# Expert weights of a PEER layer built for groups of 16 tokens instead of 8, in single one-hot tiles of twice the size and with a third PSUM bank

## The chip, the cores and the metric

The kernel runs on one core of one Trainium2 chip. The metric is the device time of one execution in microseconds (us), as the median of several runs. Engines: PE is TensorE (matmul; PEld is its weight load), DVE is VectorE, ACT is ScalarE, POOL is GpSimd, SP is SyncE, which issues the loads. Each engine works through its own queue in order; which order that is, a scheduler decides when the program is built, from the order in the source, the buffers and its own estimates.

## What is computed

One layer of a hybrid decoder for 256 tokens of width 1024. First an attention part, then the PEER part that the change touches: 8 heads choose 16 experts each out of 16384 for every token, and expert `e` adds `weight * gelu(h . u_e) * v_e`:

```
e_idx = jnp.take_along_axis(cand_idx, pos, axis=-1)
g = jax.nn.softmax(g_s, axis=-1)
u = u_emb[e_idx]
act = jax.nn.gelu(jnp.einsum('btd,bthkd->bthk', hc, u).astype(jnp.float32), approximate=False)
return jnp.einsum('bthk,bthkd->btd', (g * act).astype(h.dtype), v_emb[e_idx])
```

The kernel gathers nothing. It forms all 16384 products with U, multiplies each by its weight (zero for nearly all), and sums all 16384 rows of V with that. An expert's number is a pair (i1, i2) of 0 to 127; "row j" below is the set of 128 experts with i2 = j, and there are 128 rows.

## The kernel before

**Up to 240 us**: attention, projections, product keys. Then three stages follow one another on PE.

**The U stage (lines 920 to 954, 240 to 643 us)** takes the 128 rows of U. For row j, `take()` (line 119) gives the row's matrix in two parts: ACT makes `hi` (line 106) and DVE `lo` (line 108) from the loaded `raw` tile, three rows ahead at most, because `hi` and `lo` have three buffers each. PE runs 16 matmuls (lines 942 and 943, eight of 512 and eight of 256 columns) into one bank: `pa` (two buffers), `c1`, `c2` or `c3` in turn. ACT then copies half of the bank to `gt` (line 948), DVE adds the other half (line 949), and ACT applies gelu: straight into the store for tokens that have no weights yet (line 951), and in `gt` for those that have, which DVE then multiplies into the store (lines 953, 954). The store (`storeA`, `storeB`) holds 128 rows of 256 tokens.

**The weights** are built inside the U stage, from row J0 = 32 on, by `weights(g, j)` (line 879) for NQ = 8 tokens at a time, 32 groups in all, one every 2.8 rows. DVE makes two one-hot tiles by comparing an iota with the chosen numbers (`o1`, line 889; `og`, line 890). ACT makes `ol`, one copy per token with the low part of the weight as scale (line 892); these copies read `og`. Only when all of them are through does DVE multiply `og` in place by the high part (line 893). PE then multiplies, for each token, `o1` with `og` and with `ol` (lines 899 and 900, here called the products): 128 by 128 weights per token. Four tokens fill a bank (a quad), taken from `pb`, which has two. Each quad is emptied by DVE for rows that are done (line 905, it multiplies them into the store) and by ACT for the rest (line 907). `o1`, `og` and `ol` have two buffers each.

**The V stage (lines 961 to 996, 643 to 988 us)** takes the 128 rows of V. Each row of the store is split by ACT (`wh`, line 916) and DVE (`wl`, line 917) in `split_row`, whose tiles take the places of `o1`, `og` and `ol` in turn, so that six rows can be split ahead. PE runs 12 matmuls of 512 columns per row (`mm3`, lines 126 to 128). Between rows 4 and 12, eight loads of `w_ada` pass through the same `raw` buffers, and DVE sums them (line 983). The last three rows (125 to 127) are kept for the tail (lines 999 to 1039), which also forms the final norm.

While `sides` (line 759) has work left, DVE also runs the routing of the tokens (lines 761 to 854), up to row 31. What the order of the work around the change rests on is one line, which says at which rows a group is due:

```
while gdone < T // NQ and gdone < (j - J0 + 1) * (T // NQ) / (122 - J0):
```

Of the kernel before, what the change touches and what calls it, by code (L numbers as in the profile page):

```python
# [8 lines left out]
FR = mybir.dt.float32r  # L9
HT = mybir.dt.float16  # L10
# [6 lines left out]
T = 256  # L17
# [3 lines left out]
NEG = -1.0e30  # L21
SENT = -3.0e38
GSCALE = 32768.0
NQ = 8
BUCKET_START = [0, 1, 2, 3, 4, 5, 6, 7, 8, 9, 10, 11, 12, 13, 14, 15, 16, 23, 32, 46, 64, 91, 128, 182]
CAND_N = [16 // (a + 1) for a in range(16)]
CAND_OFF = [sum(CAND_N[:a]) for a in range(16)]
# [14 lines left out]
def hybrid_kernel(ctx, tc, io, out):  # L42
# [3 lines left out]
    def pool(name, bufs=1, stack=ctx, **kw):  # L46
        return stack.enter_context(tc.tile_pool(name=name, bufs=bufs, **kw))
# [6 lines left out]
    def bank(tag, bufs=1):  # L54
        return psum.tile([128, 512], FT, tag=tag, name=tag, bufs=bufs)
# [4 lines left out]
    def bank_b():  # L60
        return bank("pb", 2)
# [26 lines left out]
    def raw_tile():  # L88
        return st.tile([128, 1024], FT, tag="raw", name="raw", bufs=4)
# [66 lines left out]
    for part in (1, 0):  # L156
        for c in range(8):
            w = first_w[part, c] = w0.tile([128, 1024], FT, tag="wada", name="wada", bufs=8)
# [512 lines left out]
    for db in range(8):  # L671
# [4 lines left out]
        for c in range(8):  # L676
            w = slice(c * 128, c * 128 + 128)
# [59 lines left out]
    for c in range(8):  # L737
        w = slice(c * 128, c * 128 + 128)
# [125 lines left out]
    ph = pool("ph")  # L864
# [6 lines left out]
    def pieces(j0, j1):  # L871
        if j0 < SPL:
            yield storeA, j0, j0, min(j1, SPL)
        if j1 > SPL:
            yield storeB, max(j0, SPL) - SPL, max(j0, SPL), j1
# [3 lines left out]
    def weights(g, j):  # L879

        t0 = NQ * g
        sh = [128, NQ // 2, 128, 2]
        o1, og, ol = [ph.tile(sh, HT, tag=n, name=n, bufs=2) for n in ("o1", "og", "ol")]

        def of(x):
            return x[:, t0:t0 + NQ].rearrange("p (a b) -> p a b", b=2)[:, :, None, :].to_broadcast(sh)

        ii = iota[:, None, :, :].to_broadcast(sh)
        nc.vector.tensor_tensor(o1, ii, of(i1T), op=OP.is_equal)
        nc.vector.tensor_tensor(og, ii, of(i2T), op=OP.is_equal)  # L890
        for q in range(NQ):
            nc.scalar.activation(ol[:, q // 2, :, q % 2], og[:, q // 2, :, q % 2], AF.Copy, scale=glT[:, t0 + q:t0 + q + 1])  # L892
        nc.vector.tensor_tensor(og, og, of(ghT), op=OP.mult)
        for q0 in range(0, NQ, 4):
            w = bank_b()
            for q in range(4):
                qs = slice(q * 128, q * 128 + 128)
                a, b = (q0 + q) // 2, (q0 + q) % 2
                nc.tensor.matmul(w[:, qs], o1[:, a, :, b], og[:, a, :, b], start=True, stop=False)  # L899
                nc.tensor.matmul(w[:, qs], o1[:, a, :, b], ol[:, a, :, b], start=False, stop=True)  # L900
            wv = w.rearrange("p (q i) -> p i q", q=4)
            tq = slice(t0 + q0, t0 + q0 + 4)
            for s, a, lo_, hi_ in pieces(0, j):
                dst = s[:, a:a + hi_ - lo_, tq]
                nc.vector.scalar_tensor_tensor(dst, wv[:, lo_:hi_, :], 1.0 / GSCALE, dst, op0=OP.mult, op1=OP.mult)
            for s, a, lo_, hi_ in pieces(j, 128):
                nc.scalar.activation(s[:, a:a + hi_ - lo_, tq], wv[:, lo_:hi_, :], AF.Copy, scale=1.0 / GSCALE)

    def row(j):
        return storeA[:, j, :] if j < SPL else storeB[:, j - SPL, :]  # L910

    def split_row(j):

        w = ph.tile([128, 2, T], FR, tag=("o1", "og", "ol")[j % 3], name="w", bufs=2)
        wh, wl = w[:, 0, :], w[:, 1, :]
        nc.scalar.activation(wh, row(j), AF.Copy)
        nc.vector.tensor_tensor(wl, row(j), wh.bitcast(FT), op=OP.subtract)
        return wh, wl

    for j in range(128):  # L920
# [6 lines left out]
        if j == J0:  # L927
# [3 lines left out]
            storeB = sb_pool.tile([128, 128 - SPL, T], FT, name="storeB")  # L931
        while gdone < T // NQ and gdone < (j - J0 + 1) * (T // NQ) / (122 - J0):
            weights(gdone, j)
            gdone += 1
            done = NQ * gdone
        if j == 126:
            first_rows = [split_row(0), split_row(1)]
        hi, lo = take()
        ps = bank(("pa", "c1", "pa", "c2", "c3")[j % 5], 2 if j % 5 in (0, 2) else 1)
        for c in range(8):  # L940
            w = slice(c * 128, c * 128 + 128)
# [18 lines left out]
    tail = []  # L960
    for j in range(128):
        wh, wl = split_row(j) if j > 1 else first_rows[j]
        hi, lo = take()

# [11 lines left out]
        if 4 <= j < 12:  # L976
            c = j - 4
            w = raw_tile()
# [28 lines left out]
    w = slice(512, 1024)  # L1007
    residual(acc[3], 1, w, x2[:, 1, w])
    for i, (tt, a, n) in enumerate(TAIL):
        w = slice(a, a + n)  # L1010
# [84 lines left out]
```

## Time and profile before

| | |
|---|---|
| median of 3 runs | 1009.87 us (1008.82 to 1010.7) |
| the profiled execution | 1007.38 us, of which its span is 1005.6 us |
| PE busy | 970.1 us (96%) in 5693 matmuls |
| DVE busy | 778.0 us (77%) |
| ACT busy | 635.0 us (63%) |
| loads | 192.78 MB on SP's queue, 58.7% of the 16 DMA engines |
| chain that ended last | PE 63%, DVE 8%, DMA 2%, ACT 2% |
| mean granted TensorE clock | 0.995 |

The span runs from the first to the last instruction; the execution's own time has 1.8 us more around it. A matmul's duration reaches past the start of the next one, since matmuls are pipelined: how fast PE works is read from start to start, and its busy share only says that it was not left waiting for long.

### The profile page before, as it was taken

What the parts mean: (1) busy time and instruction counts of PE and PEld (TensorE: products, weight loads), DVE (VectorE), ACT (ScalarE), POOL (GpSimd) and SP (SyncE); (2) the same over time, 40 slices, a digit from 0 to 9 for tenths busy, and PEclk for the clock granted to TensorE, in tenths of its full rate; (3) what the DMA queues carried; (4) which work ended last, traced back from release to release, by engine and by line L of the source; (5) the groups of instructions that cost most, each with busy time, mean ns of one, the idle gap of its engine ahead of it and who ended that gap; (6) DMA issues with size and microseconds to landing.
All of it is one profiled execution on the core that took longest, in us unless ns stands there. A gap on an engine that the chain in (4) does not pass through costs nothing.

```text
span 1005.6 us, 16222 instructions
## 1 busy us (share of the span) xinstructions
PE 970.1 (96%) x5693; PEld 826.4 (82%) x5693; DVE 778.0 (77%) x1597; ACT 635.0 (63%) x1419; POOL 23.4 (2%) x62
## 2 busy tenths in 40 slices
PE   8899999899899999999999999999999999999996
PEld 6777888898778888888888888887888888888885
DVE  5869979799999988888889898667555555555556
ACT  4565765545556699988889787545445554554453
POOL 0000210003000000000000000000000000000000
PEclk9999999999999999999999999999999999999998
DMA  8964766453455555555555555678655666566551
GB/s 340 391 235 151 252 248 192 164 169 127 150 188 167 186 159 161 168 168 175 164 166 167 167 168 171 236 257 280 204 192 190 193 201 191 190 193 198 194 190 63
DMA packets 54996, 195.15 MB, mean 194 GB/s; under 512 B 6097, under 2 KB 8193, under 8 KB 54530
## 3 DMA queue, kind: packets, MB, share of 16 engines
q1 hardware_dynamic: 54594, 192.78, 58.7%
q10 hardware_dynamic: 320, 1.34, 0.3%
q8 instruction: 45, 0.74, 0.3%
q14 instruction: 37, 0.30, 0.1%
HBM read 191.97 MB, written 2.12 MB: 193 GB/s over the span
## 4 chain that ended last, share of the span: by engine, by line
PE 63%; DVE 8%; DMA 2%; ACT 2%; issue 1%; DVEq 0%; ACTq 0%
PE c L942 11%; PE c L127 10%; PE c L126 10%; PE c L128 10%; PE pa L942 8%; PE c L943 6%; PE pa L943 4%; DVE lo L108 2%; PE pb L899 1%; PE pb L900 1%; DMA raw<-w_ada 1%; ACT hi L106 1%; DVE gt L949 1%; DMA raw<-V 0%; ACT ol L892 0%
## 5 line engine op out<-in xcount | busy, mean ns | idle before, releaser
L108 DVE TENSOR_TENSOR lo<-raw,hi 128x1024 fp32r<-128x1024 f32 x296 | 361.5, 1222 | 170.2 <-ACT hi L106 169.4
L106 ACT ACTIVATE hi<-raw 128x1024 fp32r<-128x1024 f32 x299 | 316.1, 1058 | 222.5 <-PE c L128 151.6
L942 PE MATMUL c<-h,hi 128*128 128x512 f32 x608 | 218.2, 399 | 1.2 <-ACT hi L106 1.2
L127 PE MATMUL c<-lo,w 128*128 128x512 f32 x509 | 198.6, 390 | 1.1 <-DVE lo L108 1.0
L126 PE MATMUL c<-hi,w 128*128 128x512 f32 x509 | 198.4, 390 | 0.0
L128 PE MATMUL c<-hi,w 128*128 128x512 f32 x509 | 198.0, 389 | 0.0
L943 PE MATMUL c<-h,lo 128*128 128x256 f32 x608 | 158.3, 281 | 5.0 <-DVE lo L108 5.0
L942 PE MATMUL pa<-h,hi 128*128 128x512 f32 x416 | 151.7, 399 | 1.0 <-ACT hi L106 1.0
L942 PEld LDWEIGHTS c<-h,hi 128*128 128x128 f32 x608 | 112.8, 188 | 22.8 <-ACT hi L106 2.1
L943 PEld LDWEIGHTS c<-h,lo 128*128 128x128 f32 x608 | 114.0, 189 | 12.6 <-DVE lo L108 7.2
L127 PEld LDWEIGHTS c<-lo,w 128*128 128x128 f32 x509 | 95.5, 188 | 23.0 <-DVE lo L108 3.1
L126 PEld LDWEIGHTS c<-hi,w 128*128 128x128 f32 x509 | 95.5, 188 | 20.4 <-ACT hi L106 0.7
L128 PEld LDWEIGHTS c<-hi,w 128*128 128x128 f32 x509 | 95.5, 188 | 19.8
L943 PE MATMUL pa<-h,lo 128*128 128x256 f32 x416 | 108.6, 281 | 1.0 <-DVE lo L108 1.0
L942 PEld LDWEIGHTS pa<-h,hi 128*128 128x128 f32 x416 | 78.0, 188 | 15.4 <-ACT hi L106 1.4
L892 ACT ACTIVATE ol<-og,glT 128x128 f16<-128x128 f16 x256 | 88.0, 435 | 0.1
L943 PEld LDWEIGHTS pa<-h,lo 128*128 128x128 f32 x416 | 78.1, 189 | 5.8 <-DVE lo L108 2.3
L126 PE MATMUL pa<-h,hi 128*128 128x256 f32 x240 | 70.5, 294 | 4.6 <-ACT h L254 3.3
L128 PE MATMUL pa<-h,lo 128*128 128x256 f32 x240 | 68.4, 285 | 0.7 <-DVE lo L108 0.7
L127 PE MATMUL pa<-h,hi 128*128 128x256 f32 x240 | 68.6, 286 | 0.0
L948 ACT ACTIVATE gt<-c 128x256 f32<-128x256 f32 x76 | 29.0, 381 | 36.5 <-PE c L942 36.2
L126 PEld LDWEIGHTS pa<-h,hi 128*128 128x128 f32 x240 | 46.2, 193 | 6.5 <-ACT h L254 3.6
(284 smaller groups left out, 1380.5 us busy)
## 6 DMA issues: line engine op xcount, KB each, us to landing
raw<-U SPq DMA_DIRECT2D x128, 512.0 KB, 3.5
raw<-V SPq DMA_DIRECT2D x128, 512.0 KB, 4.2
wada<-w_ada SPq DMA_DIRECT2D x40, 512.0 KB, 6.5
raw<-wqk SPq DMA_DIRECT2D x19, 512.0 KB, 5.8
raw<-wq SPq DMA_DIRECT2D x16, 512.0 KB, 4.0
raw<-wv SPq DMA_DIRECT2D x8, 512.0 KB, 8.3
raw<-wo SPq DMA_DIRECT2D x8, 512.0 KB, 4.7
raw<-w_ada SPq DMA_DIRECT2D x8, 512.0 KB, 4.6
```

The lines of the kernel that those rows point to most:

```text
L106: nc.scalar.activation(hi, raw, AF.Copy)
L108: lo_eng.tensor_tensor(lo, raw, hi.bitcast(FT), op=OP.subtract)
L126: nc.tensor.matmul(ps, lh, rh, start=first, stop=False)
L127: nc.tensor.matmul(ps, lh, rl, start=False, stop=False)
L128: nc.tensor.matmul(ps, ll, rh, start=False, stop=last)
L892: nc.scalar.activation(ol[:, q // 2, :, q % 2], og[:, q // 2, :, q % 2], AF.Copy, scale=glT[:, t0 + q:t0 + q + 1])
L899: nc.tensor.matmul(w[:, qs], o1[:, a, :, b], og[:, a, :, b], start=True, stop=False)
L900: nc.tensor.matmul(w[:, qs], o1[:, a, :, b], ol[:, a, :, b], start=False, stop=True)
L942: both = [lambda: nc.tensor.matmul(ps, hi[:, w], hcat[:, c].rearrange("p a t -> p (a t)"), start=(c == 0), stop=(c == 7)), lambda: nc.tens ...
L943: lambda: nc.tensor.matmul(ps[:, T:], lo[:, w], hh[:, c, :], start=False, stop=False)]
L948: nc.scalar.activation(gt, ps[:, T:], AF.Copy)
L949: nc.vector.tensor_tensor(gt, gt, ps[:, :T], op=OP.add)
```

## The change

NQ goes from 8 to 16, so there are 16 groups, one every 5.6 rows, each with 16 copies by ACT and one of each of DVE's three instructions, of 2048 elements instead of 1024. `o1`, `og` and `ol` are twice as large and have one buffer each instead of two, so they take the same room. A group now has four quads, and the third of them goes to bank `c0` instead of `pb`: `pb`, `pb`, `c0`, `pb`. In the V stage `split_row` has one buffer for each of its three tags, so three rows can be split instead of six.

```
-NQ = 8
+NQ = 16
...
-        o1, og, ol = [ph.tile(sh, HT, tag=n, name=n, bufs=2) for n in ("o1", "og", "ol")]
+        o1, og, ol = [ph.tile(sh, HT, tag=n, name=n, bufs=1) for n in ("o1", "og", "ol")]
...
         for q0 in range(0, NQ, 4):
-            w = bank_b()
+            w = bank("c0") if q0 == 8 else bank_b()
...
     def split_row(j):
 
-        w = ph.tile([128, 2, T], FR, tag=("o1", "og", "ol")[j % 3], name="w", bufs=2)
+        w = ph.tile([128, 2, T], FR, tag=("o1", "og", "ol")[j % 3], name="w", bufs=1)
```

The queues of the engines move with it. ACT's queue at the first group, where `ol` are the copies, `gt` and `hi` the work for the U rows, and `storeA` and `storeB` the store. Before:

```order
L951 ACTIVATE storeA<-gt 128x256
L892 ACTIVATE ol<-og,glT 128x128 x8
L948 ACTIVATE gt<-pa 128x256
L106 ACTIVATE hi<-raw 128x1024
L892 ACTIVATE ol<-og,glT 128x128
L951 ACTIVATE storeA<-gt 128x248
L953 ACTIVATE gt<-gt 128x8
L892 ACTIVATE ol<-og,glT 128x128 x2
```

After the change, from the same instruction on:

```order
L951 ACTIVATE storeA<-gt 128x256
L948 ACTIVATE gt<-pa 128x256
L892 ACTIVATE ol<-og,glT 128x128 x16
L951 ACTIVATE storeA<-gt 128x240
L953 ACTIVATE gt<-gt 128x16
L106 ACTIVATE hi<-raw 128x1024
L948 ACTIVATE gt<-c_4126 128x256
```

The eight copies stood ahead of the `gt` of the row in `pa`, and on PE the first products 14 matmuls behind that row. Now all sixteen stand behind that `gt`, in one piece, with the next `hi` behind them, and on PE the products stand 32 matmuls, which is two rows, behind that row.

ACT's queue near the end of the U stage, some rows around row 115. Before, the copies of a group are spread in pieces of at most four:

```order
L948 ACTIVATE gt<-c_7418 128x256
L106 ACTIVATE hi<-raw 128x1024
L951 ACTIVATE storeB<-gt 128x24
L953 ACTIVATE gt<-gt 128x232
L892 ACTIVATE ol<-og,glT 128x128 x4
L948 ACTIVATE gt<-pa 128x256
L106 ACTIVATE hi<-raw 128x1024
```

After the change, at the fifteenth group of sixteen:

```order
L948 ACTIVATE gt<-c_7368 128x256
L892 ACTIVATE ol<-og,glT 128x128 x16
L951 ACTIVATE storeB<-gt 128x16
L953 ACTIVATE gt<-gt 128x240
L951 ACTIVATE storeB<-gt 128x16
L953 ACTIVATE gt<-gt 128x240
L106 ACTIVATE hi<-raw 128x1024
```

The whole group's copies now stand between one row's `gt` and the next `hi`. On PE the group's products stand 30 matmuls behind the last one of the row in `c_7368`.

PE's queue in the rows behind the last products of the sixteenth and last group (`c_7723`, `pa` and `c_7779` are the banks of three rows that follow each other). Before, behind the last group, one row follows the other:

```order
L943 MATMUL c_7764<-h,lo 128x256
L942 MATMUL c_7764<-h,hi 128x512
L942 MATMUL pa<-h,hi 128x512
L943 MATMUL pa<-h,lo 128x256 x2
L942 MATMUL pa<-h,hi 128x512
```

After the change:

```order
L943 MATMUL pa<-h,lo 128x256
L942 MATMUL pa<-h,hi 128x512
L942 MATMUL c_7723<-h,hi 128x512
L942 MATMUL pa<-h,hi 128x512
L942 MATMUL c_7779<-h,hi 128x512
L943 MATMUL c_7723<-h,lo 128x256 x2
L942 MATMUL c_7723<-h,hi 128x512
```

The first matmuls of the next two rows now stand ahead of the second matmul of row `c_7723`.

## Rows read from the trace of the kernel before

**Rows 1.** Busy time by stretch: us; PE, PEld, DVE, ACT, POOL; granted clock; DMA share, GB/s.
```profile
240.00:260.00 20.00, 16.02 (x89) 12.83 (x88) 19.73 (x132) 9.69 (x19) 3.86 (x2) 1.00 0.34 106
340.00:380.00 40.00, 39.89 (x280) 34.45 (x280) 34.55 (x67) 38.88 (x114) 0.00 (x0) 1.00 0.59 178
500.00:540.00 40.00, 40.00 (x282) 34.94 (x281) 35.41 (x62) 34.35 (x107) 0.00 (x0) 1.00 0.53 169
645.00:985.00 340.00, 338.87 (x1487) 278.40 (x1486) 203.17 (x256) 170.38 (x250) 0.00 (x0) 1.00 0.64 207
```
**Rows 2.** Timeline of PE: a U row, the first and last product behind it, the next row.
```profile
472.61 0.39 PE L942 MATMUL c<-h,hi 128*128 128x512 f32 x1
...
475.43 0.23 PE L899 MATMUL pb<-og,o 128*128 128x128 f16 x1
475.50 0.22 PE L900 MATMUL pb<-ol,o 128*128 128x128 f16 x1
...
476.33 0.48 PE L942 MATMUL c<-h,hi 128*128 128x512 f32 x1
```
**Rows 3.** Timeline of PE: the second group's products, and the row ahead of them.
```profile
352.97 0.28 PE L943 MATMUL pa<-h,lo 128*128 128x256 f32 x1
353.31 0.23 PE L899 MATMUL pb<-og,o 128*128 128x128 f16 x1
```
**Rows 4.** Timeline of ACT: copies, gt and hi, twice.
```profile
344.35 2.50 ACT L892 ACTIVATE ol<-og,glT 128x128 f16<-128x128 f16 x8
346.71 0.36 ACT L948 ACTIVATE gt<-pa 128x256 f32<-128x256 f32 x1
346.97 1.05 ACT L106 ACTIVATE hi<-raw 128x1024 fp32r<-128x1024 f32 x1
347.92 0.44 ACT L892 ACTIVATE ol<-og,glT 128x128 f16<-128x128 f16 x1
...
472.89 0.36 ACT L948 ACTIVATE gt<-pa 128x256 f32<-128x256 f32 x1
...
474.11 0.30 ACT L951 ACTIVATE storeA<-gt 128x136 f32<-128x136 f32 x1
474.31 0.29 ACT L953 ACTIVATE gt<-gt 128x120 f32<-128x120 f32 x1
474.50 1.31 ACT L892 ACTIVATE ol<-og,glT 128x128 f16<-128x128 f16 x4
```
**Rows 5.** Groups by line, shapes kept apart: count, busy us, mean ns, idle before.
```profile
L890 DVE TENSOR_TENSOR og<-iota,i2T 128x1024 f16<-128x1024 f16 x32 | 21.9, 684 | 0.0
...
L845 DVE TENSOR_TENSOR m<-eq,x 128x2048 bf16<-128x2048 bf16 x2 | 2.4, 1220 | 0.0
```
**Rows 6.** Timeline of DVE: the product of the third group and what follows.
```profile
352.56 0.69 DVE L893 TENSOR_TENSOR og<-og,ghT 128x1024 f16<-128x1024 f16 x1 [0.91 <-ACT ol L892]
353.46 1.23 DVE L108 TENSOR_TENSOR lo<-raw,hi 128x1024 fp32r<-128x1024 f32 x1 [0.21 <-ACT hi L106]
```
**Rows 7.** Timeline of PE: a row that waits for its hi.
```profile
335.25 0.39 PE L942 MATMUL pa<-h,hi 128*128 128x512 f32 x1
335.48 0.39 PE L942 MATMUL c<-h,hi 128*128 128x512 f32 x1
336.89 0.51 PE L942 MATMUL pa<-h,hi 128*128 128x512 f32 x1 [1.02 <-ACT hi L106]
```
**Rows 8.** Waits from 340 to 640 us: total us, times, longest.
```profile
ACT storeA L907 <- DVE storeA L905: 7.0, 17, 0.6
```
**Rows 9.** Timeline of DVE in the V stage, beside the loads of w_ada.
```profile
678.34 1.22 DVE L108 TENSOR_TENSOR lo<-raw,hi 128x1024 fp32r<-128x1024 f32 x1 [1.37 <-ACT hi L106]
679.48 1.27 DVE L983 SCALAR_TENSOR_TENSOR late<-raw,sc,late 128x1024 f32<-128x1024 f32 x1
680.68 0.75 DVE L917 TENSOR_TENSOR w<-storeA,w 128x256 fp32r<-128x256 f32 x2
```
**Rows 10.** Timeline of PE: the two V rows of 679 and 685 us.
```profile
679.95 0.40 PE L128 MATMUL c<-hi,w 128*128 128x512 f32 x1
...
685.53 0.43 PE L126 MATMUL c<-hi,w 128*128 128x512 f32 x1
686.72 0.50 PE L127 MATMUL c<-lo,w 128*128 128x512 f32 x1 [0.76 <-DVE lo L108]
```
**Rows 11.** Timeline of ACT: the last w and the last hi of the V stage.
```profile
980.80 0.40 ACT L916 ACTIVATE w<-storeB 128x256 fp32r<-128x256 f32 x1
...
987.99 1.06 ACT L106 ACTIVATE hi<-raw 128x1024 fp32r<-128x1024 f32 x1 [1.66 <-PE c L128]
```

## The prediction

> **What bounds the kernel now.** I read the busy time by stretch first, then PE's timeline, then the two engines that feed it. From 340 us to the end of the V stage PE is almost never left alone [rows 1]: 39.89 of 40 us, 40.00 of 40, 338.87 of 340. Busy time is no proof with pipelined matmuls, so the pace is read from start to start. A U row of 16 matmuls takes 475.43 - 472.61 = 2.82 us, 0.353 per pair, and the 16 products behind it take 476.33 - 475.43 = 0.90 us, next row at once [rows 2]. The stretch holds nothing but such work, and the one wait that I see near the products is 353.31 - 352.97 = 0.34, where 0.12 would be normal: 0.2 us too much [rows 3]. So PE's amount of work sets this time, and the change takes none of it away: there are as many products and as many U rows. What PE is made to wait for anywhere in this stretch is lost for good; what DVE or ACT save there is worth nothing. ACT and DVE have little to spare, 38.88 and 34.55 of 40 us at the start of the weights, 34.35 and 35.41 later [rows 1].
>
> **What the change removes.** It halves the number of DVE's three instructions, 96 to 48. One of 1024 two-byte elements takes 684 ns and one of 2048 takes 1220 ns [rows 5], so each pair saves 0.15 us and 48 pairs save 7.1 us of DVE. PE waits for DVE only those 0.2 us, so I book them at 0.2, no more. [...]
>
> **What it adds: a longer chain between a U row and the products.** ACT's copies are as many as before and cost 0.30 us each (8 in 2.50, 4 in 1.31 [rows 4]). But a group's product (line 893) waits for all of its copies, and they are now 16. Behind a U row's end on PE the chain is: 0.28 until `gt` starts (472.61 to 472.89 [rows 2, 4]), 0.26 until ACT's next instruction (346.71 to 346.97 [rows 4]), 16 copies at 2.50 + 8 x 0.30 = 4.90, DVE's product 1.22 [rows 5], and two hand-overs of 0.06 (352.56 + 0.69 to 353.31 [rows 3, 6]): 6.78 us. Where the copies stand straight behind a `gt`, PE gets to the products too soon:
> - Group 1: the products stand two rows behind that `gt`'s row, 5.64 us. PE waits 1.1.
> - Group 15: they stand 30 matmuls behind it, 5.64 - 0.35 = 5.29. PE waits 1.5.
> - Groups 10 and 11: a `hi` (0.95 [rows 4]) stands ahead of the copies, so 7.73, and the products stand 43 matmuls behind, 7.58. PE waits 0.15 each, 0.3.
>
> The same copies stand ahead of the `hi` of a later row. In groups 3 and 4 four and three of them, then two gelus (0.39 [rows 4]), then eleven more stand between a row's `gt` and the `hi` of the row that is three rows on. Counted from the end of the row ahead: 2.82 + 0.54 + 1.2 + 0.39 + 3.3 + 1.05 + 0.06 = 9.36, and 9.06 with three. PE wants that `hi` after three rows, 8.46: waits of 0.9 and 0.6, 1.5 together. In groups 5, 6, 8 and 9 the same sum ends within 0.1 of 8.46, or the copies stand where there is a row more: 0.
>
> Group 2 has the pattern of group 9, but DVE comes to it with the routing and the first group's quads behind it. If DVE has caught up PE waits 0; if its `og` is a `lo` late (1.23 [rows 6]), 1.3. I take 0.7, the middle.
>
> Group 16: the first matmuls of the next two rows now stand ahead of the rest of a row. The second one's `hi` has to wait for a buffer, and so for the end of the row before and its `gt`: 0.54 + 1.05 + 0.06 = 1.65, against two matmuls of 0.23 (335.25 to 335.48 [rows 7]). PE waits 1.2. The trace has this pattern once, at 335 us, and there the start came 1.41 after the one before, 1.2 too late [rows 7].
>
> **The third bank.** Quads go `pb`, `pb`, `c0`, `pb`. The fourth needs the first bank back, which DVE and then ACT have to empty, one after the other: ACT's copies already wait for DVE's, 17 times, 7.0 us, 0.6 at most [rows 8]. Between third and fourth quad PE has five to nine U matmuls. Nearly covered: 0 to 0.3 in each of 16 groups; I take 0.6 in all.
>
> **One buffer instead of two.** Next group's `o1` stands in DVE's queue behind the fourth quad's emptying, so it waits for nothing: 0. In the V stage `w` of row k may be split once row k - 3 is through, which is when `hi` of row k gets its buffer too; two rows of PE time cover `hi` and `lo` and the two `w` halves. It shows where a sum of `w_ada` stands between `lo` and `wl` of the same row, as with row 13: `lo` ends at 679.56, its `wl` would come at 681.1 [rows 9], and PE wants it at 679.95 [rows 10], a wait of 1.2. But two rows later PE stands waiting from 685.53 + 0.23 to 686.72 for a `lo` that hangs on a load [rows 10], so the delay is swallowed: 0, at most 1.2. At the end the `w` of row 127, done at 980.80 before, now has to follow the `hi` of 987.99 [rows 11]: 0.3, between 0 and 0.5.
>
> SP's queue of loads and POOL's keep their order through all of this; only the last stores of the output are paired otherwise, after the last wait.
>
> **The sum.** 1.1 + 1.5 + 0.3 + 1.5 + 0.7 + 1.2 + 0.6 - 0.2 + 0 + 0.3 = 7.0 us slower. Against the profiled execution (1007.38, 2.5 below the median of the runs) that is 1014.4; against the median 1009.87 it is **1016.9 us**, +0.7%. A measurement of this kernel can tell about 0.2%, 2 us, from no change.
>
> **The rivals.**
> 1. *DVE's saving counts.* If DVE set the stage's time, 7.1 us would go: 1002.8. For it: DVE is 86 to 89% busy there. Against: PE's pace [rows 1, 2]; a DVE that held PE up would show in PE's gaps. [...] Chance 0.02.
> 2. *Not slower: the copies are ready in time.* The place is ACT's piece of 16 copies. If they followed each other every 0.20 us, the chain would be 5.2, and groups 1 to 4, 10, 11 and 15 would not wait; group 16, the third bank and the tail leave 1.2 + 0.6 + 0.3 - 0.2 = 1.9: 1011.8, not to be told from no change. The point that decides is the copies' pace: at 0.24 group 15 still waits 0.6. For it: the scheduler put the products where by its estimates they are ready. Against: 0.30 in both rows [rows 4]. Chance 0.11.
> 3. *ACT never catches up.* ACT is at 38.88 of 40 us when the weights start [rows 1]. If every group holds PE up by the 1.1 of group 1, that is 16 x 1.1 = 18: 1028. Against: over a period of 5.6 rows ACT's work is unchanged and was done in time before; 34.35 of 40 us later on. Chance 0.05.
> 4. *One buffer delays the V stage* by the 1.2 of row 13 at each of eight `w_ada` sums, on top of the forecast: 10 more, 1027. Against: the order has `wl` ahead of `lo` again from row 14 on. Chance 0.02.
>
> **How the numbers follow.** The forecast has 0.8: terms as above, 3 to 13 us. Its low end has groups 1, 15 and 16 alone, 3.8, less some luck; its high end takes group 2 at 1.3, the fourth quad at 0.3 in all groups (4.8), row 13 at 1.2 and the tail at 0.5, 12.6. Reaching into rival 2 on one side and short of the rarest ends on the other, the range is 1011.3 to 1022.0 us. Slower: nearly all of the forecast with rivals 3 and 4, 0.87. Within 0.2%: rival 2, 0.11. Faster: rival 1, 0.02. [...]
>
> **What would show it.** PE's gaps: about 1.1 ahead of the first products, 0.6 to 1.3 at groups 2 to 4, 1.5 ahead of the products of group 15, 1.2 behind those of group 16, released by DVE's line 893 or ACT's `hi`; little at groups 5 to 9. DVE's three instructions at 1.22, about 7 us less busy in all. The V stage as long as before. I am wrong if PE's stretch from the first product to the end of U is no longer than before, or if the gaps sit at the fourth quads or in every group alike.

## The result, and the profile after

| | before | after |
|---|---|---|
| median of 5 runs each | 1008.82 us | 1015.9 us (1014.83 to 1016.66) |
| ratio to before | 1 | 1.0072, 95% interval 1.006 to 1.0083 |
| profiled execution, its span | 1007.38, 1005.6 us | 1014.83, 1013.0 us |
| U stage, from the start of its first matmul to the start of its last | 403.43 us | 410.43 us |
| V stage, from the start of its first matmul to the end of its last | 352.9 us | 352.9 us |
| mean granted TensorE clock | 0.995 | 0.996 |

The kernel became slower by 0.72%, and the forecast was 1016.9. Of the 7.4 us between the two profiled spans, 7.0 are in the U stage; 0.2 lie ahead of it and 0.2 behind the V stage. The page's busy times of after:

```profile
PE 972.1 (96%) x5693; PEld 826.1 (82%) x5693; DVE 768.6 (76%) x1549; ACT 636.6 (63%) x1418; POOL 23.4 (2%) x62
```

DVE is 9.4 us less busy than the 778.0 of before, with 48 instructions fewer. By line (count, busy us, mean ns, idle before and its cause), the first row from the kernel before and the rest from after, against [rows 5]:

```profile
L893 DVE TENSOR_TENSOR og<-og,ghT 128x1024 f16<-128x1024 f16 x32 | 22.0, 688 | 2.9 <-ACT ol L892 2.2
...
L893 DVE TENSOR_TENSOR og<-og,ghT 128x2048 f16<-128x2048 f16 x16 | 19.6, 1226 | 46.5 <-ACT ol L892 46.5
L889 DVE TENSOR_TENSOR o<-iota,i1T 128x2048 f16<-128x2048 f16 x16 | 19.5, 1220 | 0.0
L890 DVE TENSOR_TENSOR og<-iota,i2T 128x2048 f16<-128x2048 f16 x16 | 19.5, 1220 | 0.0
```

So DVE's saving is there: these three lines take 58.6 us, and 65.8 before. Line 893 has something else: after the change DVE stood idle for 46.5 us ahead of it, once in each of the 16 groups, for ACT's copies. In the kernel before that was 2.2 us, in 7 of 32 groups. Busy time by stretch (PE, PEld, DVE, ACT, POOL; granted clock; DMA share), against [rows 1]:

```profile
340.00:380.00 40.00, 39.09 (x267) 34.02 (x266) 31.45 (x56) 34.70 (x100) 0.00 (x0) 1.00 0.51 173
500.00:540.00 40.00, 39.96 (x270) 34.81 (x270) 33.81 (x56) 34.09 (x101) 0.00 (x0) 1.00 0.53 170
652.00:992.00 340.00, 338.71 (x1487) 278.44 (x1486) 203.16 (x256) 171.10 (x251) 0.00 (x0) 1.00 0.62 207
```

PE lost most of a microsecond in the first of them, nothing that shows in the second, nothing in the V stage. The places are in PE's timeline. Group 1, with ACT's and DVE's rows that belong to it:

```profile
345.62 0.39 ACT L948 ACTIVATE gt<-pa 128x256 f32<-128x256 f32 x1 [1.14 <-PE pa L942]
345.90 4.83 ACT L892 ACTIVATE ol<-og,glT 128x128 f16<-128x128 f16 x16
...
350.74 0.40 PE L942 MATMUL c<-h,hi 128*128 128x512 f32 x1
...
350.76 1.23 DVE L893 TENSOR_TENSOR og<-og,ghT 128x2048 f16<-128x2048 f16 x1 [3.83 <-ACT ol L892]
...
350.98 1.05 ACT L106 ACTIVATE hi<-raw 128x1024 fp32r<-128x1024 f32 x1
...
352.04 0.22 PE L899 MATMUL pb<-og,o 128*128 128x128 f16 x1 [0.91 <-DVE og L893]
```

Sixteen copies in one piece of 4.83 us, the product, then PE: 1.30 us between two starts where 0.23 is normal. The other large waits, at groups 3, 15 and 16 in this order:

```profile
383.81 0.40 PE L942 MATMUL c<-h,hi 128*128 128x512 f32 x1
384.88 0.49 PE L942 MATMUL pa<-h,hi 128*128 128x512 f32 x1 [0.67 <-ACT hi L106]
...
598.54 0.39 PE L942 MATMUL c<-h,hi 128*128 128x512 f32 x1
600.00 0.39 PE L943 MATMUL pa<-h,lo 128*128 128x256 f32 x1 [1.07 <-DVE lo L108]
...
629.94 0.40 PE L942 MATMUL pa<-h,hi 128*128 128x512 f32 x1
631.60 0.50 PE L942 MATMUL c<-h,hi 128*128 128x512 f32 x1 [1.26 <-ACT hi L106]
```

The `lo` that PE waits for at group 15 stands on DVE behind both one-hot instructions:

```profile
596.15 1.22 DVE L889 TENSOR_TENSOR o<-iota,i1T 128x2048 f16<-128x2048 f16 x1
597.29 1.22 DVE L890 TENSOR_TENSOR og<-iota,i2T 128x2048 f16<-128x2048 f16 x1
...
598.72 1.22 DVE L108 TENSOR_TENSOR lo<-raw,hi 128x1024 fp32r<-128x1024 f32 x1
```

To add up the small ones too, I took every pair of PE matmuls that follow each other from 340 us to the end of U, and counted the time from start to start less the normal one in these two traces (0.235 us behind a matmul of 512 columns, 0.117 behind one of 256, 0.057 behind a product). By what stands behind the gap, in us ("rest" is the products that follow a product, and the U matmul behind the last of them):

| | first product of a group | products behind U matmuls inside a group | U matmul with `hi` | U matmul with `lo` | rest | sum |
|---|---|---|---|---|---|---|
| before | 0.55 | none | -0.25 | 1.93 | -0.39 | 1.84 |
| after | 2.02 | 0.62 | 3.48 | 3.31 | -0.56 | 8.87 |

Two matmuls of the routing lie in this stretch too; how they are counted moves the sum of either kernel by the same 0.1 to 0.2 us, and not the difference. That is 7.03 us: 1.5 at the first products, 0.6 at the later ones (a group is now cut in two pieces on PE, with four to ten U matmuls between them), 5.1 at U matmuls whose `hi` or `lo` is late.

### The profile page after: what moved, and what is told of

Its sections match the earlier page's. It is cut to its first block, busy times and chain, and to the rows that moved or that the text cites. A ratio compares the mean times of both kernels' runs of the same rounds, so it can differ in the third digit from the quotient of the medians.

```text
span 1013.0 us, 16125 instructions
## 1 busy us (share of the span) xinstructions
PE 972.1 (96%) x5693; PEld 826.1 (82%) x5693; DVE 768.6 (76%) x1549; ACT 636.6 (63%) x1418; POOL 23.4 (2%) x62
## 4 chain that ended last, share of the span: by engine, by line
PE 59%; DVE 10%; ACT 3%; DMA 2%; issue 2%; ACTq 0%; DVEq 0%
PE c L127 10%; PE c L128 10%; PE c L126 10%; PE c L942 10%; PE pa L942 7%; PE c L943 5%; PE pa L943 4%; DVE lo L108 3%; ACT ol L892 1%; DMA raw<-w_ada 1%; PE pb L899 1%; PE pb L900 1%; DMA raw<-V 1%; ACT hi L106 1%; DVE gt L949 1%
## 5 line engine op out<-in xcount | busy, mean ns | idle before, releaser
L892 ACT ACTIVATE ol<-og,glT 128x128 f16<-128x128 f16 x256 | 78.9, 429 | 3.1 <-DVE og L890 3.1
L893 DVE TENSOR_TENSOR og<-og,ghT 128x2048 f16<-128x2048 f16 x16 | 19.6, 1226 | 46.5 <-ACT ol L892 46.5
```

## The experiments

The theory at the start was the prediction's: a group's 16 copies on ACT hold up the products and the `hi` queued behind them; single buffers and the third bank are worth next to nothing. The rival causes were these two: the single buffers, and the third bank. All kernels were timed in five rounds beside the kernel before. U is the U stage in the profiled execution, measured as in the table of the result. Each edit also lets the scheduler order the queues anew, so a run shows what the edit and the new order do together.

| kernel | median us | ratio to before, 95% | U, us |
|---|---|---|---|
| 16 tokens, two banks | 1017.18 | 1.0089 (1.0065 to 1.0113) | 411.21 |
| 8 tokens, one buffer | 1011.34 | 1.0030 (1.0017 to 1.0042) | 406.07 |
| 16 tokens, `ol` by DVE | 1011.93 | 1.0026 (1.0014 to 1.0038) | 405.89 |
| 16 tokens, products a row later | 1014.25 | 1.0058 (1.0036 to 1.0080) | 409.07 |
| 16 tokens, short rows | 1015.05 | 1.0057 (1.0043 to 1.0070) | 410.41 |
| 16 tokens, short rows, two buffers | 1011.41 | 1.0022 (1.0013 to 1.0031) | 405.46 |
| 8 tokens, short rows, two buffers | 1009.50 | 1.0009 (0.9997 to 1.0020) | 403.37 |
| 16 tokens, copies in two pieces | 1015.74 | 1.0063 (1.0049 to 1.0077) | 410.70 |
| 16 tokens, short rows, two buffers, four banks | 1006.84 | 0.9992 (0.9982 to 1.0001) | 402.39 |
| 16 tokens, second `ol` | 1015.28 | 1.0076 (1.0063 to 1.0089) | 410.53 |
| 16 tokens, second `og` | 1011.05 | 1.0033 (1.0021 to 1.0045) | 406.44 |
| 16 tokens, second `og`, four banks | 1006.83 | 0.9989 (0.9979 to 0.9998) | 402.48 |

**Two banks instead of three.**

```
-            w = bank("c0") if q0 == 8 else bank_b()
+            w = bank_b()
```

> Runs of 16 as in the changed kernel, but all four quads of products use the two banks of before. Theory (the 7 us are the chain of 16 ACT copies and the work queued behind it; the third bank is worth nothing): as the changed kernel, 1014.5 to 1017, and the fourth quad's products start at most 0.3 us later in each group. Rival A (the third bank carries its part: without it the fourth quad waits for a bank in each of the 16 groups): up to 16 x 0.3 = 4.8 us more, 1018 to 1021. Rival B (the third bank is what disturbs the U rows' own banks): back towards 1009.

U took 0.8 us more than in the changed kernel, the time lies just above the theory's 1017, and the two ratios' intervals overlap. As the theory had it, the third bank neither carries nor disturbs much.

**One buffer, with runs of 8.**

```
-        o1, og, ol = [ph.tile(sh, HT, tag=n, name=n, bufs=2) for n in ("o1", "og", "ol")]
+        o1, og, ol = [ph.tile(sh, HT, tag=n, name=n, bufs=1) for n in ("o1", "og", "ol")]
...
-        w = ph.tile([128, 2, T], FR, tag=("o1", "og", "ol")[j % 3], name="w", bufs=2)
+        w = ph.tile([128, 2, T], FR, tag=("o1", "og", "ol")[j % 3], name="w", bufs=1)
```

> The kernel before with runs of 8, and its one change is one buffer instead of two for the one-hot tiles and for the V rows' tiles. Theory (length of the chain): eight copies are done 2.5 us after they start, so the chain stays shorter than the two U rows ahead of the products; 1008 to 1010.5, and the U stage within 1 us of the 403.4 of before. Rival (one buffer is the cause: a group's tiles are written only when the products of the last group are done): 1014 or more, with DVE's one-hot instructions waiting for PE's products. For the V rows the theory expects 352.5 us as in both kernels; the rival some 1 us more at each w_ada sum.

Between the two, and that is where the theory began to fall: the copies are as short as before (eight in 2.50 us), yet U takes 2.6 us more (the V stage 352.8, as expected). The groups by line from 340 to 652 us:

```profile
L899 PEld LDWEIGHTS <-o 128*128 128x128 f16 x256 | 24.1, 97 | 8.5 <-DVE og L893 8.1 <-issue 0.3
L893 DVE TENSOR_TENSOR og<-og,ghT 128x1024 f16<-128x1024 f16 x32 | 22.2, 693 | 33.4 <-ACT ol L892 33.1
```

Now DVE waits for the copies in 28 of 32 groups, and PE's products for DVE. The reason shows when each group's end of line 893 is set beside the start of its first product. In the kernel before, the first four groups have 0.06 to 0.22 us between the two, the fifth 2.06, all later ones 4.6 to 11.4: the weights are finished a group ahead. With one buffer it is 0.06 to 0.26 us in all 32 groups. In the changed kernel it is 0.05 to 0.45 in all 16.

**`ol` by one DVE instruction.**

```
-    glT = cst.tile([128, T], FT, name="glT")
+    glT = cst.tile([128, T], HT, name="glT")
...
-        for q in range(NQ):
-            nc.scalar.activation(ol[:, q // 2, :, q % 2], og[:, q // 2, :, q % 2], AF.Copy, scale=glT[:, t0 + q:t0 + q + 1])
+        nc.vector.tensor_tensor(ol, og, of(glT), op=OP.mult)
```

> The changed kernel with the 16 ACT copies of a group replaced by one DVE multiplication by the low weights (kept in 16 bits, so the low parts are rounded). Theory: ACT is rid of 79 us, so hi is never late (0.9 and 0.6 at groups 3 and 4, 1.4 at group 16 go); the chain from a gt to the products is about 0.7 + 2 x 1.22 and fits into two U rows of 5.64, so group 1's 1.1 goes as well; the wait at group 15 for DVE's lo (1.2) stays or grows by 1.2. 1009.5 to 1012. Rival A (the copies are not what holds PE, but the tiles' size or the order of work): stays at 1015 to 1017. Rival B (DVE, 33.8 of 40 us busy at 500 to 540, gets 1.22 us more for each 25 us and becomes the bound): above 1016.

As expected, at the upper end: the waits for `hi` and at the first products are gone (-0.06 and 0.06 us in the table's terms), and DVE, 36.48 of 40 us busy at 500 us, did not become the bound. The wait for `lo` at group 15, which I had expected to stay, went too. So with ACT rid of the copies, single buffers make no `hi` late. But the products behind U matmuls inside a group now wait 3.74 us in all. One of these, on PE, where the bank still has to be emptied:

```profile
452.81 0.39 PE L942 MATMUL pa<-h,hi 128*128 128x512 f32 x1
453.39 0.22 PE L899 MATMUL pb<-og,o 128*128 128x128 f16 x1 [0.19 <-ACT storeB L907]
```

**Products a row later in the source.** The edit is shown in part.

```
-            weights(gdone, j)
+            ready.append((gdone, weights(gdone, j)))
```

(`weights` ends behind line 893, and the products are a function of their own, called when the next row begins.)

> The changed kernel with the same instructions, but the products of a group stand one U row (2.82 us) later in the program than its one-hot tiles and copies. Theory: the chain then has one row more of cover, and the wait ahead of the first products (1.1 at group 1) goes; the hi that is late behind the copies (0.9, 0.6 and 1.4) stays, since the copies still stand in ACT's queue in one piece: 1012.5 to 1015. Rival A (the waits come from work on DVE and ACT and not from the place of the products): 1015.5 to 1017. Rival B (with one buffer, later products hold the tiles longer and the next group's one-hot tiles wait): above 1017.

The time fell within the expected range, but not for the expected reason: group 1 still waits 1.07 us, and in 9 of 16 groups, as in the changed kernel, the first product comes 0.05 or 0.06 us behind the end of line 893. So the place in the source did not set the place on PE; that the scheduler goes by its own estimates of when the products are ready fits this, and is not shown. What moved are some later waits (0.54 instead of 0.83 at group 3; 1.17 and 1.15 near the end instead of 1.22, 0.33 and 1.42).

**Two buffers with runs of 16.** A second buffer for all three tiles is 12 KB more per partition. To make room for that, the base for this has the last 32 rows of the store in 16 bits, which is 16 KB less; a third kernel has the same with runs of 8.

```
-            storeB = sb_pool.tile([128, 128 - SPL, T], FT, name="storeB")
+            storeB = sb_pool.tile([128, 128 - SPL, T], BF, name="storeB")
```

> The base for the next kernel, to make room in SBUF: the changed kernel (runs of 16, one buffer) with the last 32 of the 128 rows of activations kept in 16 bits instead of 32, so those rows are rounded. All theories: about the changed kernel's 1014 to 1017, with U's stage at 409 to 412 us between its first and its last matmul; its instructions are the same in number.

> As the run before (last 32 rows in 16 bits), with two buffers instead of one for the one-hot tiles and the V rows' tiles: runs of 16 with the buffers that runs of 8 had. New theory (the second buffer let the one-hot tiles and copies run a group ahead, so that in the kernel before the weights were ready 5 to 11 us ahead of their products; with one buffer products come 0.05 us behind the multiply): weights ready several us ahead of the products again, the waits at the products and at the late hi mostly gone, U's stage at 402 to 405 us, 1007 to 1010. Rival (the theory of the prediction: sixteen copies in one piece on ACT hold up hi and the gt whatever the buffers): waits of 0.5 to 1.4 for hi at three or four groups stay, U's stage at 407 to 410, 1012 to 1015.

> The kernel before (runs of 8, two buffers) with the last 32 rows in 16 bits: the control of the two runs before it. All theories: within 1.5 us of the kernel before, U's stage 402 to 404.5 us. Runs of 16 with two buffers have 16 groups fewer, so, if the 0.08 us behind each group is all that the groups cost PE, they come out up to 1.3 us below this one.

Base and control behave like the full kernels (410.41 beside 410.43, 403.37 beside 403.43). The second buffer gives 4.95 of the 7.0 us back. Weights are ready 6.7 to 14.6 us ahead from the fifth group on, as the new theory had it, and the long waits for `hi` are gone although ACT still makes 16 copies per group: the rival falls as it was put, "whatever the buffers". But with the second buffers the copies no longer stand in one piece either. The changed kernel has ten pieces of 16; here only group 1 has one, nearly all the others are of four or fewer, and two of them look like this on ACT:

```profile
484.61 1.30 ACT L892 ACTIVATE ol<-og,glT 128x128 f16<-128x128 f16 x4
485.78 0.36 ACT L948 ACTIVATE gt<-pa 128x256 f32<-128x256 f32 x1
486.04 1.05 ACT L106 ACTIVATE hi<-raw 128x1024 fp32r<-128x1024 f32 x1
...
487.39 1.31 ACT L892 ACTIVATE ol<-og,glT 128x128 f16<-128x128 f16 x4
```

So this run does not tell the buffers from the pieces that come with them. And 405.46 is over the new theory's 402 to 405; runs of 16 came out 2.1 us above the control with runs of 8, where up to 1.3 below had been expected. The rest is mainly group 1's 1.07, and again the products inside a group, 2.01 us. One of them on PE:

```profile
491.96 0.39 PE L942 MATMUL pa<-h,hi 128*128 128x512 f32 x1
492.52 0.22 PE L899 MATMUL pb<-og,o 128*128 128x128 f16 x1 [0.17 <-ACT storeB L907]
```

**Copies in two pieces**, with one buffer. The edit is shown in part.

```
-        for q in range(NQ):
+        for q in range(8):
...
+        for q in range(8, 16):
```

(The second loop, line 893 and the products are called when the next row begins.)

> The changed kernel (runs of 16, one buffer) with a group's 16 ACT copies in two pieces of eight: the second piece, the multiply by the high weights and the products stand one U row later in the program. Theory of the prediction (one piece of 4.9 us on ACT makes hi late): the 0.8, 0.5 and 1.4 us at groups 3, 4 and 16 shrink by half or more, U's stage 407 to 409 us, 1011.5 to 1014. Rival (one buffer is the main cause, products follow as soon as the last copy is done whatever stands between): chain and products as tight as before, 409 to 411 us, 1014 to 1017.

The time is the rival's. The waits at groups 3 and 4 went, as the theory had it, but others came (1.03 at group 1, 1.17 in group 7, 0.7 in group 15, 1.0 behind group 16), and their sum stays, 9.12 us in the table's terms beside 8.87. Cutting ACT's piece in this way is not the cure. It did not spread the copies, though: most halves are still pieces of eight, and a group's copies run within 5.1 to 7.3 us, where they took 4.8 to 6.0. So it says little on what a wide spread would do.

**Which tile needs the second buffer.** Here one tile gets it, 4 KB more, with all rows in 32 bits. For `ol`, and for `og` in the same way (`o1` alone was not tried):

```
+        o1, og, ol = [ph.tile(sh, HT, tag=n, name=n, bufs=1 + (n == "ol")) for n in ("o1", "og", "ol")]
...
+        w = ph.tile([128, 2, T], FR, tag=("o1", "og", "ol")[j % 3], name="w", bufs=1 + (j % 3 == 2))
```

> The changed kernel with a second buffer for the tile of the ACT copies alone (and the V rows that share it), 4 KB more. If what matters is that the whole chain (one-hot tile, copies, multiply) can run a group ahead, this changes nothing, since the copies read og, and og's next tile cannot be written before the products are done: U's stage 409.5 to 411 us, 1014.5 to 1017. Rival (the copies are held by their own tile): 406 to 408 us, 1011 to 1013.5.

> The changed kernel with a second buffer for og alone (and the V rows that share it), 4 KB more. The next group's og can then be written a group ahead, but its copies wait for ol, which the products hold, and its o1 too: the chain from the copies on stays as tight as with one buffer, 4.8 us of copies and 1.2 of multiply right ahead of the products. By the theory of the whole chain U's stage is 408.5 to 411 us, 1013.5 to 1017. Rival (DVE's one-hot instructions late in its queue are the cause): 406 to 408 us, 1011 to 1013.5.

`ol` as expected: nothing. `og` against my expectation and within the rival's range, in which DVE's one-hot instructions come too late in its queue: it alone gives 4.0 of the 7.0 us back. I had looked at how far the weights are ready ahead of the products, and that is still only 0.05 to 1.4 us in most groups. What changes is how the chain is spread. The ninth group in the kernel with a second `og`, where the previous group's first products start at 467.30 (the first row writes this group's `og`, into a buffer that has just come free, just as ACT begins the eighth group's copies):

```profile
452.82 1.23 DVE L890 TENSOR_TENSOR og<-iota,i2T 128x2048 f16<-128x2048 f16 x1 [0.45 <-PE pb L899]
...
471.91 0.73 ACT L892 ACTIVATE ol<-og,glT 128x128 f16<-128x128 f16 x2
472.52 0.36 ACT L948 ACTIVATE gt<-c 128x256 f32<-128x256 f32 x1
472.78 1.05 ACT L106 ACTIVATE hi<-raw 128x1024 fp32r<-128x1024 f32 x1
...
474.43 1.02 ACT L892 ACTIVATE ol<-og,glT 128x128 f16<-128x128 f16 x3
475.34 0.39 ACT L948 ACTIVATE gt<-pa 128x256 f32<-128x256 f32 x1
...
483.65 1.22 DVE L893 TENSOR_TENSOR og<-og,ghT 128x2048 f16<-128x2048 f16 x1
```

And the same group in the changed kernel, where the previous group's first products start at 476.71:

```profile
479.44 0.22 PE L899 MATMUL pb<-og,o 128*128 128x128 f16 x1
...
480.46 0.45 DVE L905 SCALAR_TENSOR_TENSOR storeA<-pb,storeA 128x284 f32<-128x284 f32 x1
...
485.49 1.22 DVE L889 TENSOR_TENSOR o<-iota,i1T 128x2048 f16<-128x2048 f16 x1
...
488.31 1.22 DVE L890 TENSOR_TENSOR og<-iota,i2T 128x2048 f16<-128x2048 f16 x1
...
489.56 4.84 ACT L892 ACTIVATE ol<-og,glT 128x128 f16<-128x128 f16 x16 [0.28 <-DVE og L890]
494.27 0.35 ACT L948 ACTIVATE gt<-pa 128x256 f32<-128x256 f32 x1
...
494.43 1.23 DVE L893 TENSOR_TENSOR og<-og,ghT 128x2048 f16<-128x2048 f16 x1 [3.57 <-ACT ol L892]
```

With one buffer `og` is written behind the emptying of the last quad, and here 7.85 us after that began. The buffer alone does not ask for that much: the last product that reads the old `og` began at 479.44, 8.87 us ahead of the new one. In the 15 groups that follow another it is 5.0 to 8.9 us; with a second `og` the tile is written 0.26 us behind the product that frees its buffer in 9 of 14 groups. So single buffers keep `og` behind the previous products, and the rest of its delay is the place that the scheduler gave it on DVE. One buffer with the one-hot instructions earlier in that queue was not tried. ACT gets the copies 12.85 us after the previous products began, all at once, and DVE stands idle behind them. With a second `og` the writing of the tile began 19 us before its copies, ACT takes them two to four at a time between one `gt` and the next, and they are through in 11.7 us without a `hi` or `lo` being late there.

**A fourth bank for the products.** The U rows give up `c1` and take turns over four banks.

```
-            w = bank("c0") if q0 == 8 else bank_b()
+            w = bank(f"c{q0 // 4 - 2}") if q0 >= 8 else bank_b()
...
-        ps = bank(("pa", "c1", "pa", "c2", "c3")[j % 5], 2 if j % 5 in (0, 2) else 1)
+        ps = bank(("pa", "c2", "pa", "c3")[j % 4], 2 if j % 4 in (0, 2) else 1)
```

> Runs of 16, two buffers, last 32 rows in 16 bits as in the run with 1011.4 us, and a fourth bank for the products: the fourth quad takes c1, which the U rows give up (they take turns over four banks instead of five). In the run with three banks the fourth quad of a group stood behind a U row and waited 0.1 to 0.3 us for the evictions of the first quad's bank. Theory A (the 2.1 us that runs of 16 cost with two buffers are that wait, some 1.7 us, and group 1's 1.07): U's stage falls from 405.5 to 403.5 to 404.5 us, 1009 to 1010.5. Rival (the wait is not the bank, or the U rows miss theirs): 405.5 us or more, 1011.4 or more.

> The changed kernel, all rows in 32 bits, with the two changes that helped put together: a second buffer for og alone (and the V rows that share it) and a fourth bank for the products, c1, with the U rows on four banks. If the two gains add (1011.05 with the second og; 4.6 us from the fourth bank with two buffers of everything), U's stage takes 402 to 404 us and the time is 1006 to 1009, the same as or a little below the kernel before with 4 KB less than its buffers. Rival (the fourth bank helps only where weights are ready 10 us ahead; with og alone doubled they are ready 0.05 to 1.4 us ahead, so the products still stand close behind the multiply): 405 to 407 us, 1009.5 to 1011.5.

The first came out below theory A's range, the second within its own: more than the 1.7 us that I had counted, U is 3.1 us shorter with short rows and two buffers, 4.0 with all rows in 32 bits and a second `og`. With the second `og` the waits inside groups were 3.04 us of the table's terms before the fourth bank, and those at the first products 1.30 (0.34 with it). Each group is now one piece of 32 matmuls on PE, at the end of which the next row follows; the rows where a group in this last kernel begins and ends:

```profile
486.50 0.40 PE L942 MATMUL pa<-h,hi 128*128 128x512 f32 x1
486.74 0.23 PE L899 MATMUL pb<-og,o 128*128 128x128 f16 x1
...
488.53 0.22 PE L900 MATMUL c<-ol,o 128*128 128x128 f16 x1
488.56 0.47 PE L942 MATMUL c<-h,hi 128*128 128x512 f32 x1
```

There are 16 such pieces where both given kernels have 32, nothing is left inside them that waits for a bank, and the sum of the table is 0.42 us, against 1.84 before and 8.87 after. Group 1's 1.07 went too: its copies now stand on ACT ahead of the next row's `gt` and not behind it, with 34 U matmuls between their start and the products instead of 28. The last kernel keeps all rows in 32 bits, has 4 KB per partition more in these tiles than both given kernels (not 4 KB less than the kernel before, as its expectation says), and with 0.9989 (0.9979 to 0.9998) it is the one version that came out ahead of the kernel before, by an amount at the edge of what can be told.

## Why the prediction was right, and where it was not

The number was right, 1016.9 against 1015.9, and so were the stage and most places; part of the cause was not.

- **PE sets the time, DVE's saving is worth nothing:** shown. DVE's three instructions take 1.22 us, and 7.2 us less in all, where 7.1 were counted; the kernel is slower.
- **Group 1, 1.1:** 1.07. **Groups 3 and 4, 0.9 and 0.6, by a late `hi`:** 0.83 and 0.54, and another 0.12 each at the products. **Groups 10 and 11, 0.15 each:** 0.18 each. These sums of rows held to 0.1 us. (The line 893 in [rows 6] is the second group's, as the sum needs it, and not the third's.)
- **Group 16, 1.2:** 1.42, and 0.33 for a `lo` ahead of it.
- **Group 15, 1.5 at its products:** mis-placed. PE waited 1.22 earlier, for a `lo` that stood behind two one-hot instructions in DVE's queue; the row that was delayed by that gave the products their time back, and they waited 0.06. I had counted what ACT's queue does there and not DVE's.
- **Group 2, 0.7 (0 to 1.3):** 0.07; DVE had caught up.
- **The fourth quad, 0.6:** 0.62. But it is small because PE's products are late anyway. Where the weights were made early, the same wait was 2.0 to 3.7 us in all.
- **One buffer in the V stage, 0:** right, 352.9 us in both. Row 13 and the row ahead of it waited 0.65 and 0.53 us for `wl`, and the stage came out as long as before. **Tail, 0.3:** 0.2.
- **One buffer in the U stage, 0:** the step that failed. The prediction said "Next group's `o1` stands in DVE's queue behind the fourth quad's emptying, so it waits for nothing: 0". It waits for nothing, but it stands behind that emptying because there is one buffer. A second `og` alone is worth 4.0 us with runs of 16; the second buffers of all three are worth 4.95 with runs of 16 (and short rows), and with runs of 8 their loss costs 2.6.

So the terms, which count waits along the queues as the change leaves them, add up to the right sum, while the text put their cause down to 16 copies in a piece. Long pieces there are, and without copies on ACT no `hi` is late (-0.06 us in the table's terms); but the second `og` alone takes nearly all of them apart, so it is the late `og` that makes them long. That the sum is right to 0.1 us is in part luck: group 2's 0.7 was hardly there, and 0.57 that no term had (0.33 at group 16, 0.24 at the products of groups 3 and 4) stood in for it, as group 15's 1.22 at a `lo` stood in for 1.5 at its products.

Two kinds of gap on PE are to be told apart. The wait for a bank repeats: with a second `og` and three banks PE waits 0.19 to 0.32 us inside 10 of 16 groups, and with the fourth bank that is gone. The waits that the missing buffer left on PE differ in size and place (1.07, 0.83, 0.54, 1.22, 1.42), and what repeats there is that products begin 0.05 or 0.06 us behind the end of line 893, in 9 of 16 groups.

The parts of the 7.0 us as the runs have them: 4.0 for the missing second `og`, and 4.0 for the missing fourth bank once that is there, which together go 1.0 beyond the kernel before. A fourth bank without the second `og` was not tried, so how the parts split in the other order is open. So is how much of the fourth bank's gain is the bank and how much the other order that came with the same edit; the waits inside groups that went with it are 3.0 us of the 4.0.

## What to carry to other kernels

When a tile doubles in size and loses its second buffer to pay for it, look at which writer can then no longer run ahead: here the cost was not that it waited, but that its whole chain moved up against its consumer and came in one piece. Look first at the tile that the rest of the chain reads: here a second buffer for that one brought 4.0 us, where second buffers for all three brought 4.95. Count the PSUM banks with the group's size too, and expect a wait for a bank to grow when the wait ahead of it is cured (0.62 us to 2.0 and more here).

## What had not been expected of the hardware

Nothing in the durations: the copies keep their pace (16 in 4.83 us, 0.30 each), DVE's instruction of 2048 two-byte elements takes 1.22 us whether it compares or multiplies (1220 and 1226 ns), and the emptying of a quad from `pb` into the last 32 rows takes ACT 267 ns on the mean of 48 with these rows in 16 bits, and 267 ns in the changed kernel with 32. What surprised is no matter of the chip but of the order that the scheduler makes: products called a row later in the source still begin 0.05 or 0.06 us behind the instruction that they wait for, in 9 of 16 groups.
